# Hybrid block on one core: the gates' product between the compression's inputs, a layout by sixteens, and later compression units

## The chip, the core and the metric

The kernel runs on one core of a Trainium2 chip. The core has a matrix engine (TensorE, PE), a vector engine (VectorE, DVE), a scalar engine (ScalarE, ACT), GpSimd (POOL) and an engine that issues transfers (SyncE, SP), each with its own queue of instructions. The metric is the time of one execution on the device, in microseconds; 2186.89 us is the median of three runs of the kernel before.

## What is computed

One block of a decoder on 512 tokens of width 2048, in float32: an RMS norm, one input projection for two kinds of attention (a dilated one and a sparse one with compressed, selected and window branches), an output projection, a SwiGLU layer and a last norm. The change touches only the start of the sparse attention: its compression and its gates.

```python
chunks = kv.reshape(B, G, nc, CMP_STRIDE, hd)          # nc = 32 chunks of 16 tokens
blocks = jnp.concatenate([chunks[:, :, i:i + n_cmp] for i in range(r)], axis=3)   # 31 blocks of 32
blocks = blocks + pe
flat = blocks.reshape(B, G, n_cmp, CMP_BLOCK * hd)
return jax.nn.silu(flat @ w1) @ w2
...
gates = jax.nn.sigmoid(g_b.reshape(B, S, N_HEADS_B, N_GATES)).transpose(0, 2, 1, 3)
```

The compression is done for keys and for values (two streams), each with two groups. `kv` there is the projection of the normed input, so the norm's factor of each token (the kernel's `r1`) multiplies it, as it does the gates' projection `g_b`.

## The kernel before

**Arithmetic.** A float32 product is made of three matmuls of rounded parts. Each weight half, 128 x 512, is split on its way: ScalarE makes the high part `wh` (line 136) and VectorE the low part `wl` (line 139). `next_half` (line 172) asks for splits three halves ahead; `wh` and `wl` have five buffers each. Weights come by SP in units of 512 KB, two halves each, into four buffers `raw` (line 108). The order of the units in memory and on SP's queue is that of `plan()` (line 43), which reads `W1_AFTER`.

**Order.** The program is written out by hand: each engine does its instructions in the order of the text. The compression's inputs are projected first (16 matmul groups into four PSUM tiles `pc`, line 307: stream s, group g is `pc[2 * s + g]`). Then TensorE makes the sums for the norm (line 211), the gates' projection `pg` (lines 316 and 317), and, in its midst, spreads the norm's factor (line 243), which ScalarE copies to `r1` (line 246).

**The stretch of the change** is `kv_group(0, True)` (line 658). It makes four projections, `ks`, `kw`, `vs`, `vw`, each in two halves (`in_unit`, lines 165 to 167; I call them ks0, ks1, kw0 ...), 8 steps of three matmuls to a half, and an evacuation behind each second half (`evac`, lines 431 to 438; `evac_v`, line 443). Between the halves stand:

- **the compression's inputs** (`kv_part`, line 330), eight pieces written here as three digits: stream, group, shift. A piece of shift 0 first multiplies `pc` by `r1` into a buffer `tmp` (line 333, VectorE). Each piece then adds the position's column, from `tmp` into `ku`, whose order is (place among sixteen, chunk) (line 341, VectorE), rounds it to `kvs` (line 343, ScalarE), and subtracts for the low part (line 328, VectorE), which runs with the next piece. `task` takes one piece at a time from the list `tasks`; `run_unit` calls it four times in each projection half, so 000, 001, 010, 011 lie in ks0 and the others in ks1.
- **the gates** (`gates_out`, line 358), called behind ks0: VectorE multiplies `pg` by `r1` (line 360), TensorE turns it in four transposes (line 363), ScalarE copies, VectorE adds the two parts (line 365), ScalarE takes the sigmoid.
- **the compression's units** (`w1_unit`, line 370), 16 in all, eight to a stream. A unit uses two weight halves with eight matmuls (lines 382 and 383). How many follow each projection half is said by `W1_AFTER`. Behind the eighth unit of a stream (number 7 and number 15, counted from 0) ScalarE copies the sums (line 386). After ten units the keys' compression is turned (line 392) and goes through Silu (line 398), after twelve it is finished (line 407).

After this stretch come the eight heads, the output projection, the SwiGLU layer and the last norm, which the change does not touch.

Of the kernel before, what the change touches and what calls it, by code (L numbers as in the profile page):

```python
# [14 lines left out]
OP = mybir.AluOpType  # L15
# [21 lines left out]
MH, ML, WH, WL = 32, 32, 16, 16  # L37


W1_AFTER = {"ks": (0, 0), "kw": (3, 3), "vs": (3, 3), "vw": (2, 2)}  # L40


def plan():
# [3 lines left out]
    for name in ("ks", "kw", "vs", "vw"):  # L47
        for half in range(2):
            p.append(("in", name, 0, half))
            for _ in range(W1_AFTER[name][half]):  # L50
                p.append(("w1", n))
# [20 lines left out]
def block_kernel(ctx: ExitStack, tc: tile.TileContext, xt, wst, wdn, smalls, wg, w2c, bias, ident_in, out):  # L72
# [3 lines left out]
    pe, act, dve, pool_e, sp = nc.tensor, nc.scalar, nc.vector, nc.gpsimd, nc.sync  # L76
# [172 lines left out]
    def tokens(*accs):  # L249
        return [[a[:, 128 * t:128 * t + 128] for a in accs] for t in range(accs[0].shape[-1] // 128)]  # L250
# [24 lines left out]
    def tmp(name="tmp"):  # L275
        return ap_.tile([128, S], F32, tag="tmp", name=name, bufs=3)
# [12 lines left out]
    pc = [ps.tile([128, 512], F32, tag=t, name="pc", bufs=2) for t in ("proj", "proj", "sc", "sc")]  # L289
# [23 lines left out]
    r1 = Rsqrt(tokens(acc[:, 0, :]), D)  # L313
    pg = ps.tile([128, 512], F32, tag="o", name="pg")
    for k in range(KB):
        pe.matmul(pg[:48, :], wgs[:, k, :, :], ah[:, k, :], start=(k == 0), stop=False, skip_group_check=True)
        pe.matmul(pg[:24, :], wgs[:, k, 0, :], al[:, k, :], start=False, stop=(k == KB - 1), skip_group_check=True)
        if k == 11:
            r1 = Spread(r1.y)()

    tasks = deque()
# [3 lines left out]
    def kv_low():  # L325
        if pend:
            l, u, h = pend.pop()
            dve.tensor_tensor(l, u, h.bitcast(F32), op=OP.subtract)

    def kv_part(s, g, v):  # L330
        if not v:
            kv_src[0] = tmp()
            dve.tensor_tensor(kv_src[0], pc[2 * s + g], r1, op=OP.mult)
        tv = kv_src[0].rearrange("p (c i) -> p i c", i=16)
        c = (SM_PK, SM_PV)[s] + 16 * v
        u = cp.tile([128, S], F32, tag="ku", name="ku", bufs=2)
        uv = u.rearrange("p (i c) -> p i c", i=16)
        n = 32 - v
        if v:
            pool_e.memset(uv[:, :, 31:], 0.0)  # L340
        dve.tensor_tensor(uv[:, :, :n], tv[:, :, v:], sm[:, c:c + 16, None].to_broadcast([128, 16, n]), op=OP.add)
        h, l = (kvs[:, s, v, :, i, g, :] for i in range(2))
        act.activation(h, uv, AF.Copy)
        kv_low()
        pend.append((l, uv, h))

    kv_src = [None]
    for s in range(2):
        for g in range(2):
            for v in range(2):  # L350
                tasks.append(lambda s=s, g=g, v=v: kv_part(s, g, v))

    def task():
        (tasks.popleft() if tasks else kv_low)()

    side_hook[0] = task

    def gates_out():
        t = tmp()
        dve.tensor_tensor(t[:48, :], pg[:48, :], r1[:48, :], op=OP.mult)  # L360
        p = ps.tile([128, 4, 128], F32, tag="misc", name="pgt")
        for b in range(4):
            pe.transpose(p[:, b, :48], t[:48, 128 * b:128 * b + 128], ident[:48, :48])
        act.activation(gates, p[:, :, :24], AF.Copy)
        dve.tensor_tensor(gates, gates, p[:, :, 24:48], op=OP.add)
        act.activation(gates, gates, AF.Sigmoid)
# [3 lines left out]
    def w1_unit(n):  # L370
        s, i = divmod(n, 8)
        if n == 0:
            hid[0] = ps.tile([128, 512], F32, tag="t", name="phid", bufs=2)
            hid[1] = ps.tile([128, 512], F32, tag="t", name="phid", bufs=2)
        p = hid[s]
        for k in range(2):
            h, l = next_half()
            for a in range(2):
                q = 4 * i + 2 * k + a
                v, r = divmod(q, 16)  # L380
                wh, wl = h[:, 256 * a:256 * a + 256], l[:, 256 * a:256 * a + 256]
                pe.matmul(p[:, :256], kvs[:, s, v, r, :, :, :], wh, start=(q == 0), stop=False, skip_group_check=True)
                pe.matmul(p[:64, :256], kvs[:, s, v, r, 0, :, :], wl, start=False, stop=(q == 31),
                          skip_group_check=True)
        if i == 7:
            act.activation(hids[:, s, :], p[:, :256], AF.Copy)
# [54 lines left out]
    def evac_v(p):  # L441
        t = tmp()
        dve.tensor_tensor(t, p, r1, op=OP.mult)
        return t
# [207 lines left out]
    def proj_block(upto=None):  # L652
        return ps.tile([128, 512], F32, tag="proj", name="pp", bufs=2)
# [4 lines left out]
    def kv_group(g, w1):  # L658
        nonlocal n1
        for name in ("ks", "kw", "vs", "vw"):  # L660
            p = proj_block()
            for half in range(2):
                in_unit(p, half)
                if w1:
                    if name == "ks" and half == 0:
                        gates_out()
                    if W1_AFTER[name][half]:
                        while tasks or pend:
                            task()
                    for _ in range(W1_AFTER[name][half]):  # L670
                        w1_unit(n1)
                        n1 += 1
                        if n1 in (10, 12):
                            next(comp[0], None)
            if name[0] == "k":
                kv[name] = evac(p, name)
            else:
                kv[name] = V()
                t = evac_v(p)
                queue.append(lambda t=t, name=name, v=kv[name]: setattr(v, "x", v_turn(t, name)))  # L680
# [13 lines left out]
    for j in range(NH):  # L694
        if j == 4:
            kv_group(1, False)
        g = j // 4
        bb = load_bias(8 + j)
        ba = load_bias(j)
        p = proj_block()  # L700
# [8 lines left out]
        p = proj_block()  # L709
# [3 lines left out]
        p = proj_block()  # L713
# [5 lines left out]
        p = proj_block()  # L719
# [5 lines left out]
        t = evac_v(p)  # L725
# [85 lines left out]
    for f in range(FB):  # L811
        qj = quad_jobs(f, ORDER if f else ORDER0)
        p = f // PH - 1
# [16 lines left out]
    def out_unit(half, tag="proj"):  # L830
        p = ps.tile([128, 512], F32, tag=tag, name="pab", bufs=2)
        c = 8 - 8 * half
        run_unit([(p, ah[:, c + k, :], al[:, c + k, :], k == 0, k == 7) for k in range(8)])
        return p
# [54 lines left out]
    for nb in range(KB):  # L889
        while "hs" not in rest and (nb == 4 and not idle() or nb == 2 and (queue or cur["s"])):  # L890
            step()
        p = out_unit(1, ("proj", "sc", "t")[nb // 2 % 3])
# [86 lines left out]
    for i in range(KB):  # L979
        nb = PASS2[i]  # L980
        p = out_unit(0)
# [269 lines left out]
```

## Time and profile before

| what | value |
|---|---|
| median of three runs | 2186.89 us (2186.75 to 2187.51) |
| the profiled execution, its own time | 2186.78 us |
| its span (first to last instruction) | 2185.0 us |
| TensorE busy | 2166.4 us, 99% |
| VectorE busy | 1568.1 us, 72% |
| ScalarE busy | 969.4 us, 44% |
| mean granted TensorE clock | 0.998 |
| first matmul of ks0, in the span | 59.52 us |
| first matmul of the first query projection | 124.50 us |

A row of a timeline gives the start and the duration in us, the engine and line, the operation, the tile that it writes and those that it reads, its shape, how many rows were merged, and in brackets how long the engine had been idle before it and what ended that. Matmuls overlap: one of 128 x 512 takes 0.39 us, and the next starts about 0.23 us after it started, so lengths of stretches are taken between starts. A row of groups gives the count, the busy time in us and the mean of one in ns, and the idle time of the engine ahead of them.

### The profile page before, as it was taken

Reading aid. Unit: us, or ns where it says so; the run is one execution under the profiler, and the core shown is the slowest. Engines: PE = TensorE matmul, PEld = TensorE weight load, DVE = VectorE, ACT = ScalarE, POOL = GpSimd, SP = SyncE. Lnnn points to the kernel's source line nnn. Section 1 sums busy time; section 2 is a strip of 40 time slices with the busy share of each in tenths; the row PEclk is TensorE's granted clock in tenths of the full one; section 3 lists DMA queues with packets and bytes.
Section 4 is the critical chain, followed back from the end, with each engine's and each line's share of the span. In section 5 each row is a group of like instructions: output and inputs, shape, how many; then the busy total and the mean of one; then the engine's idle time right before and its main releaser. Section 6 shows DMA issues by size and latency. Waiting matters only on the chain.

```text
span 2185.0 us, 35905 instructions
## 1 busy us (share of the span) xinstructions
PE 2166.4 (99%) x13856; PEld 1947.5 (89%) x13856; DVE 1568.1 (72%) x3046; ACT 969.4 (44%) x1862; POOL 43.7 (2%) x51
## 2 busy tenths in 40 slices
PE   9999999999999999999999999999999999999997
PEld 7788888888887889989899999989898999999897
DVE  6755656356667578979687777869596877778686
ACT  6544444344444255535343443435353434434356
POOL 0000000000000000000000000000000000000003
PEclk9999999999999999999999999999999999999999
DMA  6442222322224224332333333323333332333233
GB/s 223 145 138 80 80 80 68 102 87 80 68 89 154 97 97 105 121 111 97 107 107 111 92 116 106 103 93 121 111 97 107 107 112 93 116 106 103 84 125 107
DMA packets 81852, 232.04 MB, mean 106 GB/s; under 512 B 8848, under 2 KB 11536, under 8 KB 81680
## 3 DMA queue, kind: packets, MB, share of 16 engines
q1 hardware_dynamic: 80960, 228.17, 32.0%
q0 software_dynamic: 720, 1.57, 0.5%
q8 instruction: 109, 1.79, 0.3%
q14 instruction: 63, 0.52, 0.1%
HBM read 225.51 MB, written 4.19 MB: 105 GB/s over the span
## 4 chain that ended last, share of the span: by engine, by line
PE 96%; DVE 2%; ACT 1%; issue 0%; DMA 0%; SPq 0%; DVEq 0%; ACTq 0%
PE P L1010 13%; PE P L1012 13%; PE P L1011 13%; PE pp L165 6%; PE pp L167 6%; PE pp L166 6%; PE pd L167 4%; PE pd L166 4%; PE pd L165 4%; PE P L167 3%; PE P L166 3%; PE pab L166 3%; PE pab L167 3%; PE pab L165 3%; PE P L165 3%; PE pt L515 1%
## 5 line engine op out<-in xcount | busy, mean ns | idle before, releaser
L136 ACT ACTIVATE wh<-raw 128x512 fp32r<-128x512 f32 x888 | 548.5, 628 | 514.8 <-PE P L1011 174.0
L139 DVE TENSOR_TENSOR wl<-raw,wh 128x512 fp32r<-128x512 f32 x888 | 596.5, 685 | 61.8 <-ACT wh L136 61.3
L1012 PE MATMUL P<-ah,wl 128*128 128x256 f32 x1056 | 291.8, 276 | 0.3 <-DVE wl L139 0.3
L1010 PE MATMUL P<-ah,wh 128*128 128x256 f32 x1056 | 291.7, 276 | 0.0
L1011 PE MATMUL P<-al,wh 128*128 128x256 f32 x1056 | 291.7, 276 | 0.0
L165 PE MATMUL pp<-ah,wh 128*128 128x512 f32 x640 | 260.4, 407 | 0.0
L167 PE MATMUL pp<-ah,wl 128*128 128x512 f32 x640 | 250.9, 392 | 0.0
L166 PE MATMUL pp<-al,wh 128*128 128x512 f32 x640 | 250.2, 391 | 0.0
L754 DVE TENSOR_TENSOR raw<-raw 128x512 f32<-128x512 f32 x346 | 237.3, 686 | 3.4
L136 ACT ACTIVATE wh<-rawd 128x512 fp32r<-128x512 f32 x160 | 101.1, 632 | 280.5 <-PE pd L166 164.7
L1011 PEld LDWEIGHTS P<-al,wh 128*128 128x128 f32 x1056 | 198.2, 188 | 0.9
L1010 PEld LDWEIGHTS P<-ah,wh 128*128 128x128 f32 x1056 | 198.2, 188 | 0.8
L1012 PEld LDWEIGHTS P<-ah,wl 128*128 128x128 f32 x1056 | 198.2, 188 | 0.5 <-DVE wl L139 0.5
L1077 DVE TENSOR_TENSOR hs<-hs,pd 128x512 f32<-128x512 f32 x98 | 67.4, 687 | 131.5 <-PE pd L167 131.3
L167 PE MATMUL pd<-ah,wl 128*128 128x512 f32 x392 | 154.5, 394 | 0.0
L166 PE MATMUL pd<-al,wh 128*128 128x512 f32 x392 | 153.7, 392 | 0.0
L165 PE MATMUL pd<-ah,wh 128*128 128x512 f32 x392 | 152.1, 388 | 0.0
L167 PEld LDWEIGHTS pp<-ah,wl 128*128 128x128 f32 x640 | 120.2, 188 | 27.9
L165 PEld LDWEIGHTS pp<-ah,wh 128*128 128x128 f32 x640 | 120.5, 188 | 19.6
L166 PEld LDWEIGHTS pp<-al,wh 128*128 128x128 f32 x640 | 120.6, 188 | 19.4
L139 DVE TENSOR_TENSOR wl<-rawd,wh 128x512 fp32r<-128x512 f32 x160 | 109.7, 686 | 23.9 <-ACT wh L136 23.3
L504 ACT ACTIVATE e<-e,st 128x512 f32<-128x512 f32 (+1 forms) x96 | 54.1, 564 | 135.3 <-DVE st L502 135.3
(281 smaller groups left out, 4920.6 us busy)
## 6 DMA issues: line engine op xcount, KB each, us to landing
raw<-in_wst_dram SPq DMA_DIRECT2D x310, 512.0 KB, 3.5
rawd<-in_wdn_dram SPq DMA_DIRECT2D x160, 256.0 KB, 2.6
bias<-in_bias_dram SPq DMA_DIRECT2D x16, 320.0 KB, 2.9
xc<-in_xt_dram SPq DMA_DIRECT2D x16, 256.0 KB, 2.7
hs<-in_xt_dram SPq DMA_DIRECT2D x16, 256.0 KB, 5.1
fin<-in_wdn_dram SPq DMA_DIRECT2D x8, 512.0 KB, 3.6
out_dram<-hs SPq DMA_DIRECT2D x8, 256.0 KB, 2.2
out_dram<-scaled SPq DMA_DIRECT2D x3, 512.0 KB, 2.8
```

The lines of the kernel that those rows point to most:

```text
L136: act.activation(self.h, self.src(), AF.Copy)
L139: dve.tensor_tensor(self.l, self.src(), self.h.bitcast(F32), op=OP.subtract)
L165: pe.matmul(o, wh, mh, start=start, stop=False)
L166: pe.matmul(o, wh, ml, start=False, stop=False)
L167: pe.matmul(o, wl, mh, start=False, stop=stop)
L504: act.activation(et, et, AF.Exp, bias=m, scale=-1.0, accum_out=den)
L515: pe.transpose(p[:, 128 * (o + b):128 * (o + b) + 128], self.e[t][:, 128 * b:128 * b + 128], ident)
L754: return lambda: dve.tensor_tensor(o(), o(), x(), op=OP.add)
L1010: pe.matmul(o, wh, mh, start=start, stop=False, skip_group_check=True)
L1011: pe.matmul(o, wh, ml, start=False, stop=False, skip_group_check=True)
L1012: pe.matmul(o, wl, mh, start=False, stop=stop, skip_group_check=True)
L1077: dve.tensor_tensor(hs[:, nb, :], hs[:, nb, :], p, op=OP.add)
```

## The change

Three things:

1. `W1_AFTER` goes from 3 units behind kw0, kw1, vs0, vs1 and 2 behind vw0, vw1 to 3 behind kw1, 4 behind vs0 and 3 behind vs1, vw0, vw1. The weights' order in memory and on SP's queue follows.
2. The product of `pc` and `r1` is written into `tmp` by the place among sixteen, in steps of 32 elements, and the sums of line 341 then read `tmp` in order; before, the product was written in order and the sums read it in steps of 16 elements.
3. The product of `pg` and `r1` becomes a task of its own, third in the list: 000, 001, the gates' product, 010 lie in ks0, and 011 begins ks1. `gates_out` begins with the transposes.

```diff
-W1_AFTER = {"ks": (0, 0), "kw": (3, 3), "vs": (3, 3), "vw": (2, 2)}
+W1_AFTER = {"ks": (0, 0), "kw": (0, 3), "vs": (4, 3), "vw": (3, 3)}
...
     def kv_part(s, g, v):
         if not v:
             kv_src[0] = tmp()
-            dve.tensor_tensor(kv_src[0], pc[2 * s + g], r1, op=OP.mult)
-        tv = kv_src[0].rearrange("p (c i) -> p i c", i=16)
+            dve.tensor_tensor(kv_src[0].rearrange("p (i c) -> p c i", i=16),
+                              pc[2 * s + g].rearrange("p (c i) -> p c i", i=16),
+                              r1.rearrange("p (c i) -> p c i", i=16), op=OP.mult)
+        tv = kv_src[0].rearrange("p (i c) -> p i c", i=16)
...
+    gated = []
+
+    def gates_in():
+        gated.append(tmp())
+        dve.tensor_tensor(gated[0][:48, :], pg[:48, :], r1[:48, :], op=OP.mult)
+
+    tasks.insert(2, gates_in)
+
     def gates_out():
-        t = tmp()
-        dve.tensor_tensor(t[:48, :], pg[:48, :], r1[:48, :], op=OP.mult)
+        t = gated[0]
         p = ps.tile([128, 4, 128], F32, tag="misc", name="pgt")
```

## The prediction

> **What bounds the kernel now.** I read the page first, for the engine that sets the end, then TensorE's table of waits over the whole span, then the timeline of the stretch that the change touches.
>
> ```profile
> span 2185.0 us, 35905 instructions
> PE 2166.4 (99%) x13856; PEld 1947.5 (89%) x13856; DVE 1568.1 (72%) x3046; ACT 969.4 (44%) x1862; POOL 43.7 (2%) x51
> PE 96%; DVE 2%; ACT 1%; issue 0%; DMA 0%; SPq 0%; DVEq 0%; ACTq 0%
> ```
>
> TensorE is busy for 99% of the span, and 96% of the chain that ended last is its own matmuls. The change takes no matmul away. So it can win only time in which TensorE stands still, and only in the stretch between the last matmul of the compression's inputs and the first query projection. The table of waits gives these two rows there (engine and line, what ended the wait, total us, times, longest):
>
> ```profile
> PE phid L383 <- DVE wl L139: 1.6, 2, 1.0
> PE pgt L363 <- ACT kvs L343: 1.3, 1, 1.3
> ```
>
> The starts on TensorE's timeline say what each stall costs with the slow restart behind it (start, duration):
>
> ```profile
> 59.52 0.39 PE L165 MATMUL pp<-ah,wh 128*128 128x512 f32 x1
> ...
> 64.73 0.39 PE L167 MATMUL pp<-ah,wl 128*128 128x512 f32 x1
> 66.42 0.41 PE L363 MATMUL pgt<-ident,tmp 48*128 48x48 f32 x4 [1.29 <-ACT kvs L343]
> 66.76 0.50 PE L165 MATMUL pp<-ah,wh 128*128 128x512 f32 x1
> ...
> 72.33 0.39 PE L165 MATMUL pp<-ah,wh 128*128 128x512 f32 x1
> ...
> 77.78 0.28 PE L382 MATMUL phid<-wh,kvs 128*128 128x256 f32 x1
> 79.11 0.33 PE L383 MATMUL phid<-wl,kvs 128*64 128x256 f32 x1 [1.05 <-DVE wl L139]
> ...
> 83.13 0.40 PE L165 MATMUL pp<-ah,wh 128*128 128x512 f32 x1
> ...
> 88.58 0.29 PE L382 MATMUL phid<-wh,kvs 128*128 128x256 f32 x1
> ...
> 91.43 0.39 PE L165 MATMUL pp<-ah,wh 128*128 128x512 f32 x1
> ...
> 124.50 0.39 PE L165 MATMUL pp<-ah,wh 128*128 128x512 f32 x1
> ```
>
> A half of a projection (24 matmuls; ks0, ks1, kw0, kw1 and so on) takes 72.33 to 77.78 = 5.45 us. Three compression units take 88.58 to 91.43 = 2.85 us undisturbed (0.95 a unit, 0.475 each of its two weight halves), but the first three take 77.78 to 83.13 = 5.35. **The first burst loses 2.50 us.**
>
> The gates' four transposes started 0.23 (a matmul's step) + 1.46 us behind the last matmul of ks0, and ks1 began at 66.76, 1.80 us after the step at 64.96. Four transposes that nothing holds up show what they cost themselves:
>
> ```profile
> 131.35 0.60 PE L449 MATMUL pv<-ident,tmp 128*128 128x128 f32 x4
> 131.71 0.48 PE L165 MATMUL pp<-ah,wh 128*128 128x512 f32 x1
> ```
>
> That is 0.36, so **the gates lose 1.80 - 0.36 = 1.44 us**. The row names ScalarE's kvs as the releaser, but what the transposes read is VectorE's product of line 360, in these rows:
>
> ```profile
> 58.49 0.69 DVE L333 TENSOR_TENSOR tmp<-pc,r 128x512 f32<-128x512 f32 x1 [4.28 <-ACT r L246]
> ...
> 65.62 0.69 DVE L360 TENSOR_TENSOR tmp<-pg,r 48x512 f32<-48x512 f32 x1
> 67.15 0.25 DVE L365 TENSOR_TENSOR gates<-gates,pgt 128x96 f32<-128x96 f32 x1 [0.84 <-ACT gates L364]
> ...
> 76.38 0.68 DVE L431 TENSOR_TENSOR tmp<-pp,r 128x512 f32<-128x512 f32 x1
> 77.76 0.69 DVE L438 TENSOR_TENSOR ksl<-tmp,ksh 128x512 fp32r<-128x512 f32 x1 [0.70 <-ACT ksh L437]
> 78.37 0.68 DVE L139 TENSOR_TENSOR wl<-raw,wh 128x512 fp32r<-128x512 f32 x1
> ```
>
> It ends at 66.31, and 0.11 later the transposes start. VectorE is the cause of both stalls: from 58.49 it works with hardly a pause through the inputs of the compression, and the low part of the first compression weights (78.37 to 79.05) comes out of that backlog 0.06 us ahead of the matmul at 79.11.
>
> A third loss lies in the burst in which the first compression is turned:
>
> ```profile
> 105.25 0.28 PE L382 MATMUL phid<-wh,kvs 128*128 128x256 f32 x1
> ...
> 106.21 1.00 PE L392 MATMUL phidt<-ident,osb 128*128 128x64 f32 x8
> 107.01 0.36 PE L382 MATMUL phid<-wh,kvs 128*128 128x256 f32 x1
> ...
> 108.88 0.13 PEld L383 LDWEIGHTS phid<-wl,kvs 128*64 128x64 f32 x1 [0.29 <-DVE wl L139]
> ...
> 109.28 0.55 PE L407 MATMUL pcmp<-osb 128*128 128x64 f32 x4
> ```
>
> 109.28 - 105.25 = 4.03, less 0.80 for the turn and 2.85 for the units: **0.38 lost**. On ScalarE the turn's Silu loads its table there, ahead of weight splits:
>
> ```profile
> 105.87 1.28 ACT L398 ACT_TABLE_LOAD   x1
> ```
>
> All that can be had is 1.44 + 2.50 + 0.38 = 4.32 us.
>
> **The change part by part.** *The gates' product* moves ahead of the pieces 010 and 011 (stream, group, shift) on VectorE; the piece 011 then drops out of ks0 behind a weight split of ks1. Ahead of the product now stand 000, 001 and one low part. Costs:
>
> ```profile
> L328 DVE TENSOR_TENSOR kvs<-ku,kvs 128x512 fp32r<-128x512 f32 x8 | 5.5, 682 | 0.0
> L341 DVE TENSOR_TENSOR ku<-tmp,sm 128x512 f32<-128x512 f32 x4 | 4.2, 1041 | 0.1
> L341 DVE TENSOR_TENSOR ku<-tmp,sm 128x496 f32<-128x496 f32 x4 | 4.1, 1019 | 0.1
> L333 DVE TENSOR_TENSOR tmp<-pc,r 128x512 f32<-128x512 f32 x4 | 2.7, 685 | 4.3 <-ACT r L246 4.3
> ```
>
> From 58.49, even at these prices, 0.69 + 2 x 1.04 + 0.68 = 3.45 bring the product's start to 61.9 and its end to 62.6; TensorE asks for it at 64.96. The 1.44 us go whole. The transposes then start at 64.96, and the gates' sum follows 0.73 later as before (67.15 - 66.42), at 65.70. VectorE waits for that, with the piece 010 done: a pause of up to 2 us, so savings ahead of it are worth nothing. TensorE's new times: ks1 from 65.32 to 70.89, kw0 to 76.33, kw1 to 81.78.
>
> The product's buffer is the second of three instead of the third; its last reader has long gone, so that costs nothing.
>
> *The layout.* Eight sums of line 341 read in steps of 64 bytes and cost 1041 ns; now they read in order, and I take the 682 ns of line 328: 0.36 saved on each. Four products of line 333 now write in steps of 128 bytes. No row shows such a write. Nearest from below are today's 685 ns, nearest from above the sums with their stepped read, 1041; the dearest operation of this size is this one:
>
> ```profile
> L438 DVE TENSOR_TENSOR qbl<-tmp,qbh x8: 691/1360/1423, 140.9 to 613.8; 128x512 fp32r<-128x512 f32 x8
> ```
>
> I take 1041, because one operand walks in steps in both, and keep 685 and 1423 for the range. [...]
>
> Now the backlog. Behind the gates' sum (65.87) stand on VectorE, at the 0.60 us by which 0.68 operations follow each other (77.76 to 78.37): a split, 011's sum and a low part (1.8), 100 with product, sum, low part (1.04 + 1.2 = 2.24), a split, 101's sum, a low part (1.8), 110 (2.24 again), and ks' evacuation, whose product to low part takes 1.38 (76.38 to 77.76) and 0.61 more. Sum 10.07: the split that kw1's first weight half needs starts at 75.9 and ends at 76.6. Its first reader is the third matmul of kw1, at 76.33 + 0.46 = 76.79. So no stall, with 0.2 us to spare; with a free write the spare is 0.9, and with 1423 ns the two products behind the gates' sum cost 0.76 more and the stall is near 0.6.
>
> *The compression later.* Before, three projection halves stood ahead of the first unit, now four: kw1's 5.45 us lie between backlog and burst. VectorE's next work is 111's sum, two low parts and kw1's second split (till about 79.3, asked for at 79.5), and then four splits of 0.60 till 81.7, and TensorE reaches the first unit at 81.78 with a lead of four weight halves. That is the state in which the burst at 88.58 ran undisturbed. The 2.50 go whole.
>
> The burst of four (behind vs0) uses 8 weight halves in 3.8 us while VectorE makes one in 0.60: from a lead of four, the split of its last half is done at about 0.63 + 0.68 + 3 x 0.6 = 3.1 us, and asked for at 7 x 0.475 + 0.12 = 3.45. No stall. The turn of the first compression now comes behind the last unit of its burst, where long projection halves cover the Silu: the 0.38 go.
>
> *What is late next.* The copy of the hidden sums (line 386), in order on ScalarE, comes at the end of unit 7. That was the second unit of its burst; now it is the first of three.
>
> ```profile
> 96.92 0.28 PE L382 MATMUL phid<-wh,kvs 128*128 128x256 f32 x1
> ```
> ```profile
> 99.02 0.39 ACT L386 ACTIVATE osb<-phid 128x256 f32<-128x256 f32 x1 [0.33 <-PE phid L383]
> 99.30 1.14 ACT L136 ACTIVATE wh<-raw 128x512 fp32r<-128x512 f32 x2
> ```
>
> It starts 99.02 - 96.92 - 1.90 = 0.20 us behind its unit, so at 1.15 of the burst, and the next split on ScalarE 0.28 later, at 1.43. Behind it is the burst's sixth half: ScalarE ends at 2.06 (0.63 a split), VectorE at 2.8, and TensorE wants it at 5 x 0.475 + 0.12 = 2.50. **A new stall of 0.35, with the restart 0.40 us.**
>
> *Transfers* move with the units, on SP's queue. The one with least time is vs0's first: its buffer comes free with kw1's second split, near 79.3.
>
> ```profile
> 80.28 0.33 SPq L108 DMA_DIRECT2D raw<-in_wst_dram  x1
> ```
> ```profile
> 84.30 0.63 ACT L136 ACTIVATE wh<-raw 128x512 fp32r<-128x512 f32 x1 [2.27 <-DMA raw<-in_wst_dram]
> ```
>
> The same buffer took 84.30 - 80.28 = 4.0 us then, so ScalarE can split at 83.3, VectorE ends by 84.7, and vs0 wants it at 84.63 + 0.46 = 85.1. Hidden, by 0.4 us.
>
> **Sum:** -1.44 - 2.50 - 0.38 + 0.40 = **-3.92 us**. TensorE is the chain behind, so the whole shifts by that. The profiled execution took 2186.78 us (span 2185.0 and 1.78 around it); the median of the runs is 2186.89. The forecast is 2186.89 - 3.9 = **2183.0 us**.
>
> **The rivals.** *VectorE stays behind.* If the sums are dear because of the broadcast column and not of the step, they stay at 1041, and the products rise. Then four sums (011, 100, 101, 110) cost 4 x 0.36 = 1.4 more ahead of kw1's split; less the 0.2 to spare, a wait of 1.2 to 1.3 at kw1 takes the first burst's place: 2184.3. A write at 1423 alone gives 2183.6. For it: no row parts step and broadcast.
>
> *The gates wait for another thing.* The row names ScalarE; if it is right, the transposes keep their 1.3 to 1.44 us: 2184.4. Against it: kvs ended 0.57 us earlier than the transposes began, line 360 just 0.11.
>
> *No new stall.* Without the 0.40 the gain is all of the 4.32, 2182.6, and with some hundredths from one burst fewer it passes the bound of faster. Against it is the order on ScalarE.
>
> *Slower.* The stepped write itself, in the pieces 100 and 110, could be so dear that VectorE reaches kw1 later than all that is gained. Each us on a product is two us there. From 2183.0 it takes (3.9 + 0.2)/2 = 2.05 us on top of 1041, 3.1 us a product, to come out even, and 2.2 us more, a product of 5.3 us, to be 0.2% slower: 2191.3. Against it: the dearest row of this size is 1423 ns.
>
> **How the numbers follow.** A measurement of this kernel can tell about 0.2%, 4.4 us: faster is below 2182.5, slower above 2191.3. Forecast (2182.5 to 2183.7, the dearer write among it) 0.67; VectorE behind 0.13; gates' wait kept 0.05; no new stall and below 2182.5 0.12; slower 0.03. The range goes from 2182.3 to 2184.5: it takes in the two rivals above the forecast and what lies just under it. Faster 0.12, same 0.85, slower 0.03.
>
> **What would show it.** In the profile after: no wait on pgt; the sums of line 341 near 0.68 us and the products of line 333 near 1.04; no wait in the first burst; one of 0.3 to 0.4 on phid in the burst behind vs1, with the copy to osb ahead of the late split; about 61.1 us (64.98 - 3.92) from the first ks matmul to the first of qb instead of 124.50 - 59.52. I am wrong if a wait on pp appears at kw1's or vs0's start, or if the burst of four stalls.

## The result, and the profile after

The changed kernel took 2184.15 us in the median of 22 runs (2183.04 to 2185.77), the kernel before 2187.59 us in 22 runs made in turn with them. That is 3.44 us less; the ratio is 0.9983 with a 95% interval of 0.9977 to 0.9988. The profiled execution took 2183.22 us with a span of 2181.5, against 2186.78 and 2185.0.

The page of the changed kernel, its first two lines, to be held against the same two of before:

```profile
span 2181.5 us, 35906 instructions
PE 2165.6 (99%) x13856; PEld 1947.4 (89%) x13856; DVE 1566.7 (72%) x3046; ACT 968.7 (44%) x1862; POOL 43.7 (2%) x51
```

TensorE has as many matmuls and is as busy as before; what went is time in which it stood still. Its waits, in the table over the whole span (engine and line, what ended the wait, total us, times, longest; in the text the lines from 341 on have moved by 2, those from 363 on by 9):

```profile
...
PE pcmp L421 <- DVE et_h L425: 0.7, 1, 0.7
...
PE phid L392 <- DVE wl L139: 0.2, 1, 0.2
```

The wait on pgt is gone, of 1.6 us on phid 0.2 is left, and the one on pcmp, behind the stretch, stands as it did. TensorE's timeline shows the places one by one (start, duration):

```profile
56.90 1.05 PE L243 MATMUL prb<-r,ones 128*128 128x128 f32 x8
...
59.42 0.40 PE L317 MATMUL pg<-al,wgs 128*24 128x512 f32 x1
59.78 0.50 PE L165 MATMUL pp<-ah,wh 128*128 128x512 f32 x1
...
65.43 0.44 PE L372 MATMUL pgt<-ident,tmp 48*128 48x48 f32 x4
...
76.81 0.39 PE L165 MATMUL pp<-ah,wh 128*128 128x512 f32 x1
77.04 0.39 PE L166 MATMUL pp<-al,wh 128*128 128x512 f32 x1
77.38 0.50 PE L167 MATMUL pp<-ah,wl 128*128 128x512 f32 x1
...
82.53 0.28 PE L391 MATMUL phid<-wh,kvs 128*128 128x256 f32 x1
...
85.37 0.39 PE L165 MATMUL pp<-ah,wh 128*128 128x512 f32 x1
...
100.14 0.28 PE L391 MATMUL phid<-wh,kvs 128*128 128x256 f32 x1
...
102.51 0.28 PE L391 MATMUL phid<-wh,kvs 128*128 128x256 f32 x1
102.97 0.33 PE L392 MATMUL phid<-wl,kvs 128*64 128x256 f32 x1 [0.18 <-DVE wl L139]
103.38 0.89 PE L401 MATMUL phidt<-ident,osb 128*128 128x64 f32 x7
...
121.37 0.39 PE L165 MATMUL pp<-ah,wh 128*128 128x512 f32 x1
```

The first burst now takes 82.53 to 85.37 = 2.84 us, undisturbed. The gates' transposes follow ks0 without a wait. The burst of four behind vs0 takes 90.86 to 94.65 = 3.79 us, also undisturbed. The burst behind vs1 takes 100.14 to 103.38 = 3.24 us, 0.39 more than three units need: the new stall of the forecast. Its late matmul follows 0.46 us behind the one ahead of it instead of 0.12, so it is 0.34 late; the row's 0.18 is counted from the end of the overlapping matmul. On ScalarE the copy of the hidden sums (line 395 now) stands ahead of the splits, as forecast:

```profile
101.29 0.39 ACT L395 ACTIVATE osb<-phid 128x256 f32<-128x256 f32 x1 [0.55 <-PE phid L392]
101.57 2.18 ACT L136 ACTIVATE wh<-raw 128x512 fp32r<-128x512 f32 x4
```

Two waits are there that the forecast did not have. At kw1 the third matmul comes 0.34 us behind the second instead of 0.23, with a slower start behind it (the restart: the next matmul starts 0.33 us later, at 77.71, instead of 0.23). And ks0 begins 0.36 us behind the last matmul of the gates' projection instead of 0.23, and its own second matmul follows after 0.33 (60.11).

What lies ahead of this stretch varies: the spread of the norm's factor (line 243) begins between 56.30 and 57.59 us in the profiles of this study. So I measure **the way** from its first matmul to the first of the query projection. Before, the spread began at 56.77:

```profile
56.77 1.05 PE L243 MATMUL prb<-r,ones 128*128 128x128 f32 x8
```

The way was 124.50 - 56.77 = 67.73 us and is now 121.37 - 56.90 = 64.47: 3.26 us less. VectorE's side of it, as groups and as a timeline:

```profile
L333 DVE TENSOR_TENSOR tmp<-pc,r 128x512 f32<-128x512 f32 x4 | 4.4, 1101 | 4.3 <-ACT r L246 4.3
L343 DVE TENSOR_TENSOR ku<-tmp,sm 128x512 f32<-128x512 f32 x4 | 2.8, 692 | 0.1
L343 DVE TENSOR_TENSOR ku<-tmp,sm 128x496 f32<-128x496 f32 x4 | 2.7, 668 | 0.0
```
```profile
58.62 1.10 DVE L333 TENSOR_TENSOR tmp<-pc,r 128x512 f32<-128x512 f32 x1 [4.28 <-ACT r L246]
...
66.19 0.26 DVE L374 TENSOR_TENSOR gates<-gates,pgt 128x96 f32<-128x96 f32 x1 [1.41 <-ACT gates L373]
...
76.64 0.68 DVE L139 TENSOR_TENSOR wl<-raw,wh 128x512 fp32r<-128x512 f32 x1
```

The sums fell from 1041 to 692 ns, the products rose from 685 to 1101. The first product ends at 59.72 and ks0 begins at 59.78; the weight load ahead of ks0's first matmul waited 0.49 us, and the profile names this product as what ended that. VectorE then stands idle 1.41 us ahead of the gates' sum, and kw1's first low part ends at 77.32, 0.06 us ahead of the late matmul at 77.38.

### The profile page after: what moved, and what is told of

It reads as the page before. It is cut to its first block, busy times and chain, and to the rows that moved or that the text cites. A ratio compares the mean times of both kernels' runs of the same rounds, so it can differ in the third digit from the quotient of the medians.

```text
span 2181.5 us, 35906 instructions
## 1 busy us (share of the span) xinstructions
PE 2165.6 (99%) x13856; PEld 1947.4 (89%) x13856; DVE 1566.7 (72%) x3046; ACT 968.7 (44%) x1862; POOL 43.7 (2%) x51
## 4 chain that ended last, share of the span: by engine, by line
PE 97%; DVE 1%; ACT 1%; DMA 0%; issue 0%; SPq 0%; DVEq 0%; ACTq 0%
PE P L1020 13%; PE P L1019 13%; PE P L1021 13%; PE pp L165 7%; PE pp L167 7%; PE pp L166 7%; PE pd L167 4%; PE pd L166 4%; PE pd L165 4%; PE P L167 3%; PE pab L166 3%; PE P L166 3%; PE pab L165 3%; PE pab L167 3%; PE P L165 3%; PE pt L524 1%
```

## The experiments

**Theory.** VectorE has one backlog, from the norm's factor to the first splits. Its delay shows wherever TensorE first asks for a product of it, so the three parts of the change are not worth what they bring alone. **Rival:** each part has its own gain, and they add up. The first six kernels do the parts alone and by twos. All times of a way are differences of two starts on TensorE's timeline; medians are of 11 or 12 runs, beside 33 or 35 of the kernel before on the same chip (2187.32 us for the first four kernels, 2187.51 for the next four, 2187.28 for the last). Each way comes from a single profile; the changed kernel, profiled twice, gave 64.47 and 64.52. The last column is the median less that of the kernel before beside it.

| kernel | spread begins | query begins | way | way against before | median against before |
|---|---|---|---|---|---|
| before | 56.77 | 124.50 | 67.73 | | |
| gates alone | 56.63 | 126.70 | 70.07 | +2.34 | +1.35 |
| layout alone | 57.18 | 124.08 | 66.90 | -0.83 | -0.57 |
| gates and layout | 56.94 | 124.30 | 67.36 | -0.37 | +0.64 |
| later alone | 57.06 | 123.34 | 66.28 | -1.45 | -1.72 |
| gates and later | 57.06 | 122.03 | 64.97 | -2.76 | -3.17 |
| layout and later | 57.59 | 123.05 | 65.46 | -2.27 | -2.47 |
| all (the change) | 56.90 | 121.37 | 64.47 | -3.26 | -3.44 |

The parts alone don't make up the whole: 0.83 and 1.45 gained and 0.18 lost (the gates alone without what the clock cost there, worked out below) are 2.10 of the 3.26 us. One pair does add up: layout and later gain 0.83 + 1.45 = 2.28 by themselves and 2.27 together. What depends on the others is the gates' product, and with it the later units: these bring 1.45 us alone and 67.36 - 64.47 = 2.89 beside the two other parts.

**Later alone.**

```diff
-W1_AFTER = {"ks": (0, 0), "kw": (3, 3), "vs": (3, 3), "vw": (2, 2)}
+W1_AFTER = {"ks": (0, 0), "kw": (0, 3), "vs": (4, 3), "vw": (3, 3)}
```

Expected: 

> Only the order of the compression's units is changed (three behind kw1, four behind vs0, three behind vs1, vw0 and vw1); layout and gates' product as before. Theory (one backlog on VectorE, whose delay goes wherever TensorE first asks for it): the gates' wait stays (1.3 on pgt), the first burst runs undisturbed, but kw1's first low part, done at 79.05 before, is asked for at 78.24, so a wait of 0.8 on pp appears there; unit 7's copy costs 0.4. Gain 2.5 + 0.4 - 0.9 - 0.4 = about 1.6 us against before: 2186.0 where before is 2187.6. Rival (the parts add up, the later units bring their whole 2.5 us): gain 2.5, no wait at kw1.

Median 2185.6 us against 2187.32, ratio 0.9991 (0.9982 to 0.9999). TensorE's waits in the stretch:

```profile
PE pgt L363 <- ACT kvs L343: 1.3, 1, 1.3
...
PE pp L167 <- DVE wl L139: 0.7, 1, 0.7
...
PE phid L383 <- DVE wl L139: 0.2, 1, 0.2
```

The burst's wait is not gone, it has shrunk and moved: kw1 now waits 0.7 us for the split for which the burst had waited. The last row is the new stall behind vs1, which comes with the order of the units. The way is 1.45 us shorter, near the theory's 1.6 and not the rival's 2.5.

**Gates alone.**

```diff
+    gated = []
+
+    def gates_in():
+        gated.append(tmp())
+        dve.tensor_tensor(gated[0][:48, :], pg[:48, :], r1[:48, :], op=OP.mult)
+
+    tasks.insert(2, gates_in)
...
-        t = tmp()
-        dve.tensor_tensor(t[:48, :], pg[:48, :], r1[:48, :], op=OP.mult)
+        t = gated[0]
```

Expected: 

> Only the gates' product is moved; the order of units and the layout as before. Theory of one backlog: the wait on pgt goes (1.44 us earlier), but VectorE's work is the same, its split for the first burst's second half still comes at about 80.2, and so the burst, which begins 1.4 us earlier, waits 1.3 us longer: waits on phid of about 3 us, gain at most 0.3 us against before. Rival (the parts add up): gain 1.4 us.

Median 2188.67 us, ratio 1.0003 (0.9994 to 1.0012): nothing gained. The wait on pgt is gone, and the burst waits 3.1 us, as the theory had it:

```profile
PE phid L390 <- DVE wl L139: 3.1, 2, 2.3
```

The way, however, is 2.34 us longer, which no theory had. TensorE's timeline and the table of stretches (from:to, length, busy us of PE, PEld, DVE, ACT and POOL, then the granted clock, the DMA's share and GB/s) show why:

```profile
77.38 0.33 PE L390 MATMUL phid<-wl,kvs 128*64 128x256 f32 x1 [0.79 <-DVE wl L139]
...
77.78 0.28 PE L389 MATMUL phid<-wh,kvs 128*128 128x256 f32 x1
80.35 0.47 PE L390 MATMUL phid<-wl,kvs 128*64 128x256 f32 x1 [2.29 <-DVE wl L139]
80.62 0.41 PE L389 MATMUL phid<-wh,kvs 128*128 128x256 f32 x1
...
84.46 0.63 PE L165 MATMUL pp<-ah,wh 128*128 128x512 f32 x1
...
90.78 0.28 PE L389 MATMUL phid<-wh,kvs 128*128 128x256 f32 x1
```
```profile
78.00:80.00 2.00, 0.06 (x1) 0.00 (x0) 1.84 (x4) 1.66 (x4) 0.00 (x0) 0.84 0.04 8
80.00:82.00 2.00, 1.65 (x8) 1.65 (x9) 2.00 (x4) 1.75 (x5) 0.00 (x0) 0.50 0.39 41
82.00:84.00 2.00, 2.00 (x11) 2.00 (x11) 1.91 (x4) 0.61 (x2) 0.00 (x0) 0.50 0.95 305
84.00:86.00 2.00, 2.00 (x8) 1.71 (x7) 1.30 (x2) 1.10 (x2) 0.00 (x0) 0.50 0.88 340
86.00:88.00 2.00, 2.00 (x9) 1.59 (x9) 0.69 (x1) 0.63 (x1) 0.00 (x0) 0.95 1.02 360
```

The clock falls to half within the pause and stays there until about 86.2 us (the mean of 0.95 from 86 to 88): a matmul of the burst takes 0.41 us where it takes 0.28 at the full clock. Before the change the same place, the second half of the first unit, stood here:

```profile
80.31 0.33 PE L383 MATMUL phid<-wl,kvs 128*64 128x256 f32 x1 [0.52 <-DVE wl L139]
```

From there the burst went on for 83.13 - 80.31 = 2.82 us; with the gates alone it took 84.46 - 80.35 = 4.11, and kw1 took 90.78 - 84.46 = 6.32 instead of 5.45. The clock costs 1.29 + 0.87 = 2.16 of the 2.34 us. What is left is 0.18 us of a longer way: the waits only changed places, as the theory has it, and its upper end of 0.3 us gained was not reached. All 11 runs read a mean clock of 0.997 or 0.996, where 24 of the 33 of before read 0.998, which speaks for a loss of this kind in the other runs too; only one of them has a trace.

**Layout alone.**

```diff
-            dve.tensor_tensor(kv_src[0], pc[2 * s + g], r1, op=OP.mult)
-        tv = kv_src[0].rearrange("p (c i) -> p i c", i=16)
+            dve.tensor_tensor(kv_src[0].rearrange("p (i c) -> p c i", i=16),
+                              pc[2 * s + g].rearrange("p (c i) -> p c i", i=16),
+                              r1.rearrange("p (c i) -> p c i", i=16), op=OP.mult)
+        tv = kv_src[0].rearrange("p (i c) -> p i c", i=16)
```

Expected: 

> Only the layout is changed. Theory: the sums at 0.69 and the products at 1.10 us leave 0.3 us less ahead of the gates' product and about 1.2 us less ahead of the first burst; ks0 waits 0.1 (0.2 with the restart) for the first product, since its tile takes the buffer that this product reads. pgt waits about 1.0, the burst's waits sink to about 1.0. Gain 0.8 to 1.3 us against before. Rival (the layout is where the change's gain comes from): 2.5 us or more.

Median 2186.75 us, ratio 0.9992 (0.9983 to 1.0001); the way is 0.83 us shorter. The waits of the backlog are smaller, none is gone (the one on pgt fell further than expected, to 0.7):

```profile
PE phid L385 <- DVE wl L139: 1.1, 2, 0.5
...
PE pcmp L414 <- DVE et_h L418: 0.7, 1, 0.7
PE pgt L365 <- ACT kvs L345: 0.7, 1, 0.7
```

**Gates and layout, units as before.**

```diff
-W1_AFTER = {"ks": (0, 0), "kw": (0, 3), "vs": (4, 3), "vw": (3, 3)}
+W1_AFTER = {"ks": (0, 0), "kw": (3, 3), "vs": (3, 3), "vw": (2, 2)}
```

Expected: 

> The changed kernel with the old order of units (gates' product moved, new layout). Theory of one backlog: no wait on pgt, but the first burst begins at 76.8 and its second half's split comes at about 80.0 (behind the piece 111), so phid waits 2.3 to 2.7 us; kw1 begins near 82.8 instead of 83.13, and the Silu's 0.4 stays. Gain 0.2 to 0.6 us against before. Rival (the parts add up): 1.44 of the gates and about 1.0 of the layout, 2.4 us.

Median 2187.96 us, ratio 1.0001 (0.9992 to 1.001): two of the three parts together gain nothing that can be measured. The way of the profile is 0.37 us shorter, and the gates' wait has gone into the burst:

```profile
PE phid L392 <- DVE wl L139: 2.2, 2, 2.0
```

The rival's 2.4 us is out. This is the clearest evidence for one backlog. Against the layout alone the gates' move even cost 67.36 - 66.90 = 0.46 us: VectorE, whose rows in the timeline stand in the order of the text, idles 1.46 us ahead of the gates' sum, with work behind it (0.84 before the change), and the matmul that waits for the low part of the burst's second half starts 80.09 - 56.94 = 23.15 us behind the spread's first matmul instead of 79.87 - 57.18 = 22.69. Way and median differ here by about 1 us: the mean clock is 0.998 in the profiled run and 0.997 in 9 of its 11 timed ones. This mean takes in the end of the span as well, where the clock reads 0.50 in the profiles of before (2178 to 2185 us) and of the change (2176 to 2181.5). Whether a pause of 2.0 us costs those runs the clock, no trace shows, and it stays open.

**Gates and later, old layout.** The layout's lines of the changed kernel go back:

```diff
-            dve.tensor_tensor(kv_src[0].rearrange("p (i c) -> p c i", i=16),
...
+            dve.tensor_tensor(kv_src[0], pc[2 * s + g], r1, op=OP.mult)
+        tv = kv_src[0].rearrange("p (c i) -> p i c", i=16)
```

Expected: 

> The changed kernel with the old layout (gates' product moved, units later). Theory of one backlog: ks0 starts without the 0.23 us that the dearer first product costs it, but kw1's first low part ends 20.75 us behind the spread's first matmul (line 243) and is asked for at 20.14, so a wait of 0.6 on pp at kw1 instead of 0.1. Nearly as fast as the changed kernel: the way from the spread to the first query matmul 64.6 to 64.9 us (64.47 after the change, 67.73 before), gain 2.8 to 3.1 us against before. Rival (the layout's saving on VectorE is a main part): gain 2 us or less.

Median 2184.34 us, ratio 0.9983 (0.9974 to 0.9992). The way of 64.97 is 0.07 us above my range. kw1 waits 0.5 us at its first half (and 0.1 at its second, too short for the table):

```profile
PE pp L167 <- DVE wl L139: 0.5, 1, 0.5
...
PE phid L390 <- DVE wl L139: 0.2, 1, 0.2
```

So the layout is worth 64.97 - 64.47 = 0.50 us in the way: it takes most of kw1's waits and gives a part back at ks0.

**Layout and later, gates' product where it was.**

```diff
...
-    tasks.insert(2, gates_in)
...
-        t = gated[0]
+        t = tmp()
+        dve.tensor_tensor(t[:48, :], pg[:48, :], r1[:48, :], op=OP.mult)
```

Expected: 

> The changed kernel with the gates' product where it was (new layout, units later). Theory of one backlog: pgt waits 0.7 to 1.0 as with the layout alone, and in return kw1 doesn't wait: from the spread to the first query matmul 64.9 to 65.3 us, gain 2.4 to 2.8 us against before. Rival (the gates' 1.44 is lost whole): gain 1.8 us.

Median 2185.04 us, ratio 0.9989 (0.998 to 0.9998). The way of 65.46 is 0.16 us above my range: pgt waits as expected, but kw1 waits too: its first low part is earlier than before the change but still late. The matmul that waits for it starts 79.08 - 57.59 = 21.49 us behind the spread's first matmul; before, this low part ended 79.05 - 56.77 = 22.28 us behind it, and with the change it ends 77.32 - 56.90 = 20.42.

```profile
PE pgt L365 <- ACT kvs L345: 0.7, 1, 0.7
...
PE pp L167 <- DVE wl L139: 0.2, 1, 0.2
```

The gates' product, worth nothing alone, is worth 65.46 - 64.47 = 0.99 us beside the two other parts.

**The first product in order.** The next two kernels take up the dearer product.

```diff
+            if (s, g) == (0, 0):
+                dve.tensor_tensor(kv_src[0], pc[0], r1, op=OP.mult)
+            else:
...
+        tv = kv_src[0].rearrange("p (c i) -> p i c" if (s, g) == (0, 0) else "p (i c) -> p i c", i=16)
```

Expected: 

> The changed kernel, but the first of the four products (piece 000) is written in order and its two sums read in steps as before; the others stay in the new layout. Theory (ks0's first matmul waits for the first product, since its PSUM buffer is the one that this product reads): the way from the spread's first matmul to ks0's first goes from 2.88 back to 2.75 us and the restart's 0.1 goes too; the gates' product still ends by 62.6. Gain 0.23 us against the changed kernel, 64.2 us from the spread to the first query matmul. Rival (the 2.88 is the spread's own variation): no change.

The way is 64.23 us. TensorE's timeline at the two ends of the short way to ks0:

```profile
57.25 1.05 PE L243 MATMUL prb<-r,ones 128*128 128x128 f32 x8
...
60.00 0.39 PE L165 MATMUL pp<-ah,wh 128*128 128x512 f32 x1
```

That is 2.75 us, as before the change (59.52 - 56.77), where all seven kernels with a stepped first write have 2.88 (and the next kernel, whose product is 67 ns shorter, 2.81). So ks0 waits for the first product, because its PSUM buffer (tag "proj", two of them) is the one that this product reads. The median, 2183.99 us, can't tell this from the change.

**The product read in steps.**

```diff
-            dve.tensor_tensor(kv_src[0].rearrange("p (i c) -> p c i", i=16),
-                              pc[2 * s + g].rearrange("p (c i) -> p c i", i=16),
-                              r1.rearrange("p (c i) -> p c i", i=16), op=OP.mult)
+            dve.tensor_tensor(kv_src[0].rearrange("p (i c) -> p i c", i=16),
+                              pc[2 * s + g].rearrange("p (c i) -> p i c", i=16),
+                              r1.rearrange("p (c i) -> p i c", i=16), op=OP.mult)
```

Expected: 

> The changed kernel, but its four products run through their operands in the order in which they are written: both reads in steps of 64 bytes (one from PSUM, one from SBUF), the write in order; the result lies in the same place. If one price is paid per element whichever stream steps: 1.04 to 1.10 us a product, and the time of the changed kernel. If each stepped stream pays: 1.4 to 1.5 us, ks0 waits 0.4 longer for the first product and kw1 0.8 longer, 1.2 us slower than the changed kernel. If PSUM's read has no price of its own: as the first.

```profile
L333 DVE TENSOR_TENSOR tmp<-pc,r 128x512 f32<-128x512 f32 x4 | 4.1, 1034 | 4.3 <-ACT r L246 4.3
```

Two stepped reads cost 1034 ns, no more than the one of line 341 (1041), and 67 ns less than the stepped write. The way is 121.42 - 57.11 = 64.31 us; the median is 2183.73 us, ratio 0.9983 (0.9974 to 0.9992).

**The gates' sum later.** `gates_out` ends with the transposes; copy, sum and sigmoid come behind the piece 011:

```diff
-        act.activation(gates, p[:, :, :24], AF.Copy)
-        dve.tensor_tensor(gates, gates, p[:, :, 24:48], op=OP.add)
-        act.activation(gates, gates, AF.Sigmoid)
+        first = tasks.popleft()
+
+        def with_gates():
+            first()
+            act.activation(gates, p[:, :, :24], AF.Copy)
+            dve.tensor_tensor(gates, gates, p[:, :, 24:48], op=OP.add)
+            act.activation(gates, gates, AF.Sigmoid)
+
+        tasks.appendleft(with_gates)
```

Expected: 

> The changed kernel, but the gates' sum and sigmoid (ScalarE's copy, VectorE's sum) come behind the piece 011 instead of ahead of ks1's split. Theory (VectorE idles 1.41 us ahead of this sum, with work behind it, and that is what kw1's first split lacks): the idle time goes to 0.2 or less, kw1's split comes 1.2 us earlier, its wait of 0.1 with the restart goes: 64.2 to 64.3 us from the spread's first matmul to the first query matmul against 64.47 after the change. Rival (kw1's wait comes from the transfers or from ScalarE): unchanged.

VectorE's idle time ahead of the sum falls from 1.41 to 0.30 us, kw1's wait goes, and the way is 121.40 - 57.17 = 64.23 us. So kw1 lacked VectorE's time, and part of that was lost in waiting for the gates. The edit moves ScalarE's copy and sigmoid as well, but kw1 did not wait for these: with the change VectorE, once past the gates' sum, stands idle only once up to kw1's low part (0.70 us, in ks' evacuation), and it does the same here. The median is 2183.75 us, ratio 0.9987 (0.9979 to 0.9996).

```profile
67.14 0.25 DVE L378 TENSOR_TENSOR gates<-gates,pgt 128x96 f32<-128x96 f32 x1 [0.30 <-ACT gates L377]
```

**Unit 7 in the middle of its burst.**

```diff
-W1_AFTER = {"ks": (0, 0), "kw": (0, 3), "vs": (4, 3), "vw": (3, 3)}
+W1_AFTER = {"ks": (0, 0), "kw": (0, 3), "vs": (3, 3), "vw": (4, 3)}
...
-                        if n1 in (10, 12):
+                        if n1 in (9, 12):
```

Expected: 

> The changed kernel with three units behind kw1, vs0 and vs1, four behind vw0, three behind vw1, and the turn of the first compression behind nine units instead of ten: unit 7 is again the second of its burst, and the Silu still meets long projection halves. Theory (the copy of the hidden sums holds up the split of the half three further on, which is in the same burst only if unit 7 is its first): no wait on phid in the burst behind vs1; 64.0 to 64.1 us from the spread to the first query matmul, 0.4 us faster than the changed kernel. Rival (the wait moves into the burst of four, now with the first compression's end in it): unchanged or slower.

The way is 120.43 - 56.32 = 64.11 us; no wait on phid is left in the stretch:

```profile
PE pcmp L421 <- DVE et_h L425: 0.7, 1, 0.7
```

The median is 2183.53 us, ratio 0.9987 (0.9978 to 0.9995). The stall behind vs1 is the place of the copy, as the forecast had it.

**All three, and the change again beside them.** The edits of the first product, the gates' sum and unit 7 together; the other kernel is the changed one, unedited.

Expected: 

> The changed kernel with the first product in order, the gates' sum later and unit 7 in the middle of its burst. If the three waits are separate, their prices add up: 0.23 + 0.22 + 0.39 = 0.84 us less than the changed kernel, 63.6 us from the spread to the first query matmul, the stretch without any wait but that of the values' compression. If VectorE's backlog links them, less: 64.0 or more.

Expected of the change again: 

> The changed kernel itself, beside the three: 64.4 to 64.5 us from the spread to the first query matmul, a median 3.2 to 3.7 us under before.

```profile
57.51 1.05 PE L243 MATMUL prb<-r,ones 128*128 128x128 f32 x8
...
121.07 0.39 PE L165 MATMUL pp<-ah,wh 128*128 128x512 f32 x1
```

The way with all three is 63.56 us, 0.91 less than the change, where 0.84 was expected of three separate prices; no wait on pgt, pp or phid is left in the table. The change again has 120.82 - 56.30 = 64.52. The medians are 2183.05 us for the three (ratio 0.998, 0.9972 to 0.9989), 2184.0 for the change (0.9984, 0.9975 to 0.9993) and 2187.28 before. The version with all three is 0.95 us under the change in the median; the intervals of the two ratios overlap, so the medians alone don't prove it; the ways, one profile each, agree with it.

## Why the prediction was right or wrong

The forecast was 2183.0 us, 3.9 less than 2186.89, in a range of 2182.3 to 2184.5. Measured were 2184.15, and 3.44 less than the kernel before. Sign, size and place were right. The median alone would not show it: it lies above the forecast's own 2182.5 to 2183.7 and close to the times of two rivals, 2184.3 and 2184.4. But 0.70 us of the distance is the larger sample of before, which stands at 2187.59; as a gain, 3.44 is nearer to the forecast's 3.9 than to the rivals' 2.6 and 2.5. What decides between them is the trace. By the terms:

- **The first burst, -2.50.** Right: 5.35 us became 2.84.
- **The gates, -1.44.** Right in the mechanism: no wait on pgt, although the row had named ScalarE. What is left between ks0's last step (65.34) and ks1 (65.80) is 0.46, not the 0.36 of other transposes: 1.34 gained.
- **The Silu, -0.38.** Right: the turn (line 401 now) comes behind the burst, and the burst with the first compression's end takes 113.05 - 109.76 = 3.29 us, 2.85 and 0.36 for that end, with 0.08 of restart.
- **The new stall, +0.40.** Right in place and size: the matmul is 0.34 us late and the burst 0.39 longer, and the kernel with unit 7 in the middle takes it away.
- **The layout's own price.** "I take 1041" was 1101, within its bounds. What the forecast missed was the place where it is paid first. I costed the product in VectorE's backlog alone, and did not name who waits for its buffer: ks0 takes the PSUM buffer that the first product reads. That is 2.88 - 2.75 = 0.13 us of wait and 0.10 of restart. The kernel with the first product in order shows it.
- **"So no stall, with 0.2 us to spare" at kw1.** Wrong, though by little: 0.11 us of wait and 0.11 of restart. A wait on pp at kw1's start is also what the forecast had named as the sign that it is wrong; it is too short for the table of waits, but the starts show it. The two dearer products behind the gates took 2 x 0.06 more, and the gates' sum began at 66.19 instead of 65.70. Against the forecast TensorE was late itself by 76.81 - 76.33 = 0.48, VectorE by 77.32 - 76.6 = 0.7.

So 3.92 less 0.23, 0.22, 0.10 and 0.08 makes 3.29, near the 3.26 of the way. From the first ks matmul to the first of qb the forecast had about 61.1 us; it is 121.37 - 59.78 = 61.59.

Of the rivals, VectorE staying behind came in small: kw1 lost 0.22 us instead of 1.2 to 1.3, since the broadcast column costs next to nothing (the sums at 692 ns, against 682 for line 328) and the step was the price. The gates did not wait for another thing: their wait went with the product's move alone. A new stall there is, and slower the kernel is not.

The forecast named VectorE's backlog as the cause of the two larger losses, and followed it as far as kw1. What its sum does not say is that its terms hold only together: -1.44 stands there as if the gates' product earned it by itself. Alone it is worth nothing, beside the two other parts 0.99 us. The sum came out nearly right because all three parts were made.

## What to carry to other kernels

Where one engine's backlog makes another wait at several places, taking away the first wait can just lengthen the second (with the gates alone the 1.3 us on pgt went, and the burst's waits rose from 1.6 to 3.1 us): follow the backlog to the end, and judge a part of a change with and without the others. When an operation is made dearer on an engine with time to spare, look at the buffers that it reads: here ks0, which was to write one of them next, waited 0.13 us for a product of 1101 instead of 685 ns. And where a step in a layout has to be paid on one side or the other, as in these kernels, it can be moved to where fewer elements pass, here from eight sums (1041 to 692 ns each) to four products (685 to 1101).

## What the runs showed of the hardware

- **A wait cost more than its length.** With the gates alone, TensorE idled 0.79 us, made four matmuls, and idled 2.29 us; the granted clock stood at 0.50 from about 79.4 to 86.2 us, which cost 2.16 us. The mean of 0.84 from 78 to 80 us puts the halving near 79.4, some 1.3 us into the second idle time (the last matmul ahead of it ended at 78.06), the mean of 0.95 from 86 to 88 its end near 86.2. The waits before the change (1.0 and 0.5 us in the burst) and the 2.0 us in the profiled run of gates and layout left the clock at 1.00. So in this run it took no idle time longer than these two. What sets the fall off, the runs don't show.
- **A stepped float32 stream cost VectorE about the same on either side**: a write in steps of 128 bytes 1101 ns, one read in steps of 64 bytes 1041, two such reads (one from PSUM) 1034, against 682 to 692 in order, each for 128 x 512. The two step lengths were not tried on the same side.
